# Conditioning weights by feature group, small vectors in one piece: a two-block transformer kernel on one core

## The chip, the core and the metric

The kernel runs on one core of a Trainium2 chip. The core has a matrix engine (TensorE, PE in the profile), a vector engine (VectorE, DVE), an activation engine (ScalarE, ACT), a general one (GpSimd, POOL) and SyncE (SP), which only issues transfers. ACT and POOL can issue transfers as well. The metric is the device time of one execution in microseconds. Three runs of the kernel before gave 2118.53, 2122.41 and 2126.63 us; the median is 2122.41.

## The reference

The reference computes two transformer blocks over 1024 tokens of 1024 features, in float32. What the change touches is the conditioning of the first block, ahead of everything else:

```
c_act = silu(c)                                   # one row of 1024
ada = c_act @ w_ada + b_ada                       # 1024 x 3072
shift, scale, gate = split(ada, 3)
h = rms_norm(x) * (1 + scale) + shift             # every projection of block one reads h
p = h @ w_in                                      # then GLA, HGRN, stick-breaking attention
x = x + gate * (mix(p) @ w_out)
```

Block two has sliding-window attention and an mLSTM behind a causal convolution, a cross attention to 256 memory rows, and a mixture of 32 experts with a router, from about 1440 us on. Small vectors (norm weights, biases, convolution taps, router weights) are needed at several places.

## The kernel before

Tokens go through in two halves of 512. Features lie on the partitions: the half's normalised rows are transposed into eight tiles `xraw` of 128 features x 512 tokens, and each is scaled and shifted with one column of `scc` and `shc` (features on partitions, so a conditioning value is one number per partition). The products are exact to more than one matrix pass: each operand is split into a rounded high part and a remainder (`whi`, `wlo` for weights, `fs` with `hi` and `lo` for features), and `mm3` makes three matmuls of them.

The head of the kernel does the following.

- The mask temporaries (`mk`, built by POOL and VectorE in a loop) are made and released; the pool `adp` of the conditioning weights then takes that memory.
- Four tiles `xt` of 128 token rows are loaded. Each is squared and summed by ACT (`junk<-xt`), POOL makes the reciprocal root (`rstd`), VectorE scales the rows, TensorE transposes, ACT copies to `xraw`.
- The conditioning weights for shift and scale come in 16 tiles `wa` of 512 KB, in G = 2 groups of 512 features. A tile holds 128 of the 1024 inputs on its partitions. VectorE multiplies each by `cs` (silu of c) and accumulates into `acc`; TensorE then sums over the partitions with a column of ones; two small VectorE operations add the biases into `shc` and `scc` (`cols<-mm` in the profile).
- Per feature tile, ACT writes the high part, POOL scales `xraw` in place, VectorE subtracts for the low part.
- TensorE then runs the low-rank gate projection (`lr`, L705 and L706, 16 matmuls of 512 columns) and the first of the projection slabs, each 24 matmuls.

The memory rows and the next half's token rows are loaded into the same four `xt` buffers once TensorE has transposed the first ones; they are scaled on VectorE too, far ahead of their use. A projection slab (`raw`, 512 KB, two buffers) is loaded by SyncE, rounded by ACT and subtracted by VectorE. `mmb` gives one of two PSUM banks in turn, for conditioning sums, the low-rank projection and slabs alike. The conditioning gate is computed later, in front of the first output projection, from eight loads of `w_ada` into the two `raw` buffers.

The order on each engine isn't written out: a scheduler with a timeline of its own sets it from data dependences and priorities, up to the expert stage, whose order is given by hand. Each engine and each transfer queue takes its instructions in that order. A transfer also waits for the one that used its completion semaphore before (eight of them, in turn).

## Time and profile before

| | us |
|---|---|
| median of three runs | 2122.41 |
| the profiled execution | 2122.66 |
| its span | 2120.9 |
| TensorE busy | 1942.5 (92%) |
| VectorE busy | 1475.0 (70%) |
| ACT busy | 1177.2 (56%) |
| POOL busy | 689.2 (32%) |

The span is what the trace covers; 1.8 us of the profiled execution lie around it. The busy share is a mean over stages: in the first 50 us TensorE is busy for 13.15 us, in the expert stage (1500 to 2040 us) without a break. So a stage has to be read by itself, and there it counts which wait ends last. Times in rows are microseconds from the start of the span.

### The profile page before, as it was taken

Reading aid. Unit: us, or ns where it says so; the run is one execution under the profiler, and the core shown is the slowest. Engines: PE = TensorE matmul, PEld = TensorE weight load, DVE = VectorE, ACT = ScalarE, POOL = GpSimd, SP = SyncE. Lnnn points to the kernel's source line nnn. Section 1 sums busy time; section 2 is a strip of 40 time slices with the busy share of each in tenths; the row PEclk is TensorE's granted clock in tenths of the full one; section 3 lists DMA queues with packets and bytes.
Section 4 is the critical chain, followed back from the end, with each engine's and each line's share of the span. In section 5 each row is a group of like instructions: output and inputs, shape, how many; then the busy total and the mean of one; then the engine's idle time right before and its main releaser. Section 6 shows DMA issues by size and latency. Waiting matters only on the chain.

```text
span 2120.9 us, 33031 instructions
## 1 busy us (share of the span) xinstructions
PE 1942.5 (92%) x12914; PEld 1644.2 (78%) x12914; DVE 1475.0 (70%) x1955; ACT 1177.2 (56%) x1868; POOL 689.2 (32%) x554
## 2 busy tenths in 40 slices
PE   3999899999999999999999998995999999999980
PEld 2878796887777998889888897894788888888860
DVE  6476774546777754677557755745888888888865
ACT  3454552445555543465435633652777777777852
POOL 3362110035354100242004300003455555555535
PEclk8999999999998999999999999996999999999995
DMA  9211334621011253211722156454899999999956
GB/s 294 76 51 51 112 97 128 208 73 48 22 50 31 61 156 118 70 50 61 208 60 60 51 149 232 149 219 154 343 382 384 373 378 368 371 372 370 378 195 243
DMA packets 218934, 381.61 MB, mean 180 GB/s; under 512 B 50164, under 2 KB 173076, under 8 KB 193176
## 3 DMA queue, kind: packets, MB, share of 16 engines
q1 hardware_dynamic: 194520, 345.79, 47.1%
q10 hardware_dynamic: 15040, 16.89, 2.3%
q0 software_dynamic: 9216, 16.80, 2.1%
q8 instruction: 102, 1.67, 0.3%
q14 instruction: 56, 0.46, 0.1%
HBM read 356.35 MB, written 39.85 MB: 187 GB/s over the span
## 4 chain that ended last, share of the span: by engine, by line
PE 76%; DVE 8%; DMA 5%; POOL 4%; issue 4%; ACT 3%; POOLq 0%; ACTq 0%; SPq 0%; DVEq 0%; another core or an unknown queue 0%
PE mm L133 11%; PE mm L134 11%; PE mm L135 11%; PE gu L134 6%; PE gu L133 5%; PE gu L135 5%; PE yo L135 3%; PE yo L133 3%; PE yo L134 3%; PE tp L189 3%; PE tpe L189 2%; DMA xp<-u_d 1%; PE sc L1139 1%; PE sc L1168 1%; PE at L599 1%
## 5 line engine op out<-in xcount | busy, mean ns | idle before, releaser
L43 DVE TENSOR_TENSOR elo<-eraw,ehi 128x2048 fp32r<-128x2048 f32 x192 | 429.6, 2263 | 81.1 <-ACT ehi L40 81.0
L40 ACT ACTIVATE ehi<-eraw 128x2048 fp32r<-128x2048 f32 x192 | 367.1, 1913 | 18.5 <-PE yo L135 12.5
L133 PE MATMUL mm<-whi,fs 128*128 128x256 f32 x1152 | 334.2, 292 | 1.9 <-ACT whi L40 1.9
L134 PE MATMUL mm<-wlo,fs 128*128 128x256 f32 x1152 | 333.4, 290 | 0.9 <-DVE wlo L43 0.8
L135 PE MATMUL mm<-whi,fs 128*128 128x256 f32 x1152 | 330.0, 288 | 0.0
L43 DVE TENSOR_TENSOR wlo<-raw,whi 128x1024 fp32r<-128x1024 f32 x156 | 197.3, 1266 | 149.8 <-ACT whi L40 143.5
L40 ACT ACTIVATE whi<-raw 128x1024 fp32r<-128x1024 f32 x156 | 164.8, 1056 | 214.6 <-PE mm L134 89.6
L43 POOL TENSOR_TENSOR elo<-eraw,ehi 128x1024 fp32r<-128x1024 f32 x64 | 188.2, 2941 | 230.4 <-ACT ehi L40 230.4
L133 PEld LDWEIGHTS mm<-whi,fs 128*128 128x128 f32 x1152 | 224.1, 195 | 10.2 <-issue 5.5
L134 PEld LDWEIGHTS mm<-wlo,fs 128*128 128x128 f32 x1152 | 224.4, 195 | 8.4 <-issue 6.0
L135 PEld LDWEIGHTS mm<-whi,fs 128*128 128x128 f32 x1152 | 223.2, 194 | 2.4 <-issue 2.3
L133 PE MATMUL gu<-ehi,xh 128*128 128x512 f32 x512 | 208.3, 407 | 2.5 <-ACT ehi L40 2.5
L134 PE MATMUL gu<-elo,xh 128*128 128x512 f32 x512 | 205.3, 401 | 1.5 <-DVE elo L43 1.5
L133 PE MATMUL mm<-fs,whi 128*128 128x512 f32 x480 | 195.5, 411 | 7.9 <-DVE mst L43 3.3
L135 PE MATMUL gu<-ehi,xl 128*128 128x512 f32 x512 | 202.4, 395 | 0.0
L134 PE MATMUL mm<-fs,whi 128*128 128x512 f32 x480 | 195.2, 407 | 1.2 <-DVE fs L52 1.2
L135 PE MATMUL mm<-fs,wlo 128*128 128x512 f32 x480 | 194.2, 405 | 0.0
L133 PEld LDWEIGHTS mm<-fs,whi 128*128 128x128 f32 x480 | 93.0, 194 | 38.9 <-issue 8.9
L133 PEld LDWEIGHTS gu<-ehi,xh 128*128 128x128 f32 x512 | 96.9, 189 | 24.7 <-ACT ehi L40 2.9
L135 PEld LDWEIGHTS gu<-ehi,xl 128*128 128x128 f32 x512 | 96.7, 189 | 22.9
L134 PEld LDWEIGHTS gu<-elo,xh 128*128 128x128 f32 x512 | 97.0, 190 | 22.0 <-DVE elo L43 2.2
L135 PEld LDWEIGHTS mm<-fs,wlo 128*128 128x128 f32 x480 | 93.2, 194 | 23.1 <-issue 4.0
(467 smaller groups left out, 4235.7 us busy)
## 6 DMA issues: line engine op xcount, KB each, us to landing
eraw<-in_w_e_up_dram SPq DMA_DIRECT2D x64, 1024.0 KB, 8.3
eraw<-in_w_e_down_dram SPq DMA_DIRECT2D x64, 1024.0 KB, 8.8
eraw<-in_w_e_gate_dram SPq DMA_DIRECT2D x64, 1024.0 KB, 8.6
raw<-in_w_in_dram SPq DMA_DIRECT2D x92, 512.0 KB, 3.8
raw<-in_w_out_dram SPq DMA_DIRECT2D x32, 512.0 KB, 3.5
wa<-in_w_ada_dram SPq DMA_DIRECT2D x16, 512.0 KB, 5.9
fy<-y_d SPq DMA_DIRECT2D x8, 1024.0 KB, 13.5
xt<-in_x_dram SPq DMA_DIRECT2D x8, 512.0 KB, 6.6
```

Of the source, the lines that this page charges most:

```text
L40: act.activation(out=o, in_=i, func=f, **kw)
L43: (eng or dve).tensor_tensor(out=o, in0=a, in1=b, op=op)
L133: pe.matmul(out=o, lhsT=l[0], rhs=r[0], start=start, stop=False)
L134: pe.matmul(out=o, lhsT=l[0], rhs=r[1], start=False, stop=False)
L135: pe.matmul(out=o, lhsT=l[1], rhs=r[0], start=False, stop=stop)
L189: pe.transpose(o[0:s.shape[-1], j * 128:j * 128 + s.shape[0]], s, ident[0:s.shape[0], 0:s.shape[0]])
L599: pe.matmul(out=ov[:, hh, ch], lhsT=full[:, hh, ch], rhs=v(ch, hh), start=True, stop=s0 is None)
L1139: pe.matmul(out=sc[g][:, jj * 256:jj * 256 + w], lhsT=q[r, j + jj, t * 128:(t + 1) * 128], rhs=k_full[r, k0:k0 + w], start=True, stop=True)
L1168: pe.matmul(out=os_[:, hh * 64:hh * 64 + 64], lhsT=pt[:, i * 128:(i + 1) * 128], rhs=v_full[:, kt, 64 * g:64 * g + 64], start=(hd == 0 and ...
```

## The change

Inputs are laid out on the host in another form, as part of passing them in; the kernel's arithmetic is the same, only the sum over the conditioning inputs is done in another order. The parts:

- Small vectors come packed: `small` (54 columns) in the first load of SyncE, `small_mix` and `small_router` later, instead of one transfer each.
- The token rows `xt` of the first half are issued by ACT.
- The conditioning weights lie by feature group, G = 4 groups of 256 features, in 8 transfers of 1 MB with 8 KB in a row per partition. They and the token rows get high priority, and two kinds of transfers are held behind the last of them (`issue_after`).
- The shift half is summed by TensorE (weights as the stationary operand, `cs` as one column, 64 matmuls); VectorE sums the scale half alone, in pieces of 256 columns.
- Two of the four token tiles are scaled by ACT; the last two feature tiles are scaled in place by VectorE instead of POOL.
- The gate third of the conditioning weights, the mLSTM gate weights and the router weights are contiguous per load.

```diff
-            sp.dma_start(out=xt, in_=src[rows_of(h, t), :])
+            (eng or sp).dma_start(out=xt, in_=src[rows_of(h, t), :])
...
-                sp.dma_start(out=xp, in_=src[rs, cs_].rearrange("(a p) n -> p a n", p=128))
+                with tc.issue_after(ada_last[-1]) if (h, kind) == (0, 0) else nullcontext():
+                    sp.dma_start(out=xp, in_=src[rs, cs_].rearrange("(a p) n -> p a n", p=128))
...
-    cc = vec_cols(c[0], 8)
+    cc = vec("c")
...
-    G = 2
+    G = GROUPS
...
-                sp.dma_start(out=rv, in_=kview(w_ada[0])[:, k0:k0 + 2, 2048 + n * 512:2048 + (n + 1) * 512])
+                sp.dma_start(out=rv, in_=w_ada_gate[n, :, k0:k0 + 2])
...
-        x0 = load_rows(x[0], 0)
-        was = []
-        for g in range(G):
-            was.append([])
-            for i in range(8):
-                raw = adp.tile([128, 2, 1024 // G], F32, name="wa", tag="wa", bufs=8 * G)
-                sp.dma_start(out=raw, in_=w_ada[0, i * 128:(i + 1) * 128, 0:2048].rearrange(
-                    "p (a k n) -> k p a n", a=2, k=G)[g])
-                was[-1].append(raw)
+        was, ada_last = [], []
+        with tc.high_priority():
+            x0 = load_rows(x[0], 0, eng=act)
+            for g in range(G):
+                for i in range(0, 8, 4):
+                    raw = adp.tile([128, 4, 2, 1024 // G], F32, name="wa", tag="wa", bufs=2 * G)
+                    ada_last.append(sp.dma_start(out=raw, in_=w_ada[g, :, i:i + 4]).ins)
+                    was += [raw[:, k] for k in range(4)]
         xraw = []
-        for x_ in x0:
-            TS(x_, x_, rstd_of(x_, D, junk_tile()), MUL)
+        for t, x_ in enumerate(x0):
+            r = rstd_of(x_, D, junk_tile())
+            if t < 2:
+                TS(x_, x_, r, MUL)
+            else:
+                A(x_, x_, AF.Copy, scale=r)
...
             if j == 0:
-                acc = adp.tile([128, 2, 1024 // G], F32, name="acc", tag="acc", bufs=2)
+                o = mmb()
+                for jj in range(gk):
+                    for i in range(8):
+                        pe.matmul(out=o[:, jj:jj + 1], lhsT=was[k // gk * 8 + i][:, 0, jj * 128:(jj + 1) * 128],
+                                  rhs=cs[:, i:i + 1], start=(i == 0), stop=(i == 7))
+                acc = adp.tile([128, 1024 // G], F32, name="acc", tag="acc", bufs=2)
                 for i in range(8):
-                    w = was[k // gk][i]
+                    w = was[k // gk * 8 + i][:, 1]
                     if i:
                         STT(acc, w, cs[:, i:i + 1], acc, MUL, ADD)
                     else:
                         TS(acc, w, cs[:, 0:1], MUL)
-                o = mmb()
-                for a in range(2):
-                    for jj in range(gk):
-                        pe.matmul(out=o[:, a * gk + jj:a * gk + jj + 1], lhsT=acc[:, a, jj * 128:(jj + 1) * 128],
-                                  rhs=ones, start=True, stop=True)
+                for jj in range(gk):
+                    pe.matmul(out=o[:, gk + jj:gk + jj + 1], lhsT=acc[:, jj * 128:(jj + 1) * 128], rhs=ones,
+                              start=True, stop=True)
...
-            TS(xraw[k], xraw[k], scc[:, k:k + 1], MUL, shc[:, k:k + 1], ADD, eng=pool)
+            TS(xraw[k], xraw[k], scc[:, k:k + 1], MUL, shc[:, k:k + 1], ADD,
+               eng=pool if k < 6 else dve)
...
-    sp.dma_start(out=fnw, in_=final_norm_w.partition_broadcast(128))
-    for a_, v_ in ((nmx, norm_mix_2), (ncr, norm_cross_2)):
-        sp.dma_start(out=a_, in_=v_[0].rearrange("(k p) -> p k", p=128))
+    with tc.issue_after(ada_last[-1]):
+        sp.dma_start(out=fnw, in_=final_norm_w.partition_broadcast(128))
...
-        sp.dma_start(out=wr[:, :, 0:4], in_=kview(w_router_group_2[0]))
-        sp.dma_start(out=wr[:, :, 4:36], in_=kview(w_router_expert_2[0]))
-        brow = cr.tile([128, 36], F32, name="brow")
-        sp.dma_start(out=brow[:, 0:4], in_=b_router_group_2[0].partition_broadcast(128))
-        sp.dma_start(out=brow[:, 4:36], in_=b_router_expert_2[0].partition_broadcast(128))
-        nffc = cr.tile([128, 8], F32, name="nffc")
-        sp.dma_start(out=nffc, in_=norm_ffn_2[0].rearrange("(k p) -> p k", p=128))
+        sp.dma_start(out=wr, in_=w_router)
+        sm3 = cr.tile([128, sum(n for _, n in SMALL_ROUTER)], F32, name="sm3")
+        sp.dma_start(out=sm3, in_=small_router)
+        small_v.update(vecs_of(sm3, SMALL_ROUTER))
+        brow, nffc = vec("router"), vec("norm_ffn")
```

The scheduler moves instructions with it. First SyncE's queue at the start of the program; before (`xt` token or memory rows, `wa` conditioning weights, `raw` slabs, `fnw` a norm weight, `xp` token pieces for the output projection):

```order
L91 DMA cols<-in_c_dram 128x8x1
L267 DMA xt<-in_x_dram 128x1024 x4
L117 DMA raw<-in_w_in_dram 128x8x128
L91 DMA cols<-in_norm_mem_dram 128x8x1
L421 DMA wa<-in_w_ada_dram 128x2x512 x16
L117 DMA raw<-in_w_in_dram 128x8x128 x2
L864 DMA fnw<-in_final_norm_w_dram 128x1024
L866 DMA cols<-in_norm_mix_dram 128x8x1
L866 DMA cols<-in_norm_cross_dram 128x8x1
L289 DMA xp<-in_x_dram 128x2x256 x2
L886 DMA cols<-in_norm_att_out_dram 128x4x1
L887 DMA cols<-in_norm_ml_out_dram 128x4x1
```

and now:

```order
L80 DMA cols<-in_small_dram 128x54
L124 DMA raw<-in_w_in_dram 128x8x128
L425 DMA wa<-in_w_ada_dram 128x2048 x8
L877 DMA fnw<-in_final_norm_w_dram 128x1024
L297 DMA xp<-in_x_dram 128x2x256 x2
L124 DMA raw<-in_w_in_dram 128x8x128 x2
L274 DMA xt<-in_mem_dram 128x1024 x2
L274 DMA xt<-in_x_dram 128x1024 x2
L124 DMA raw<-in_w_in_dram 128x8x128
```

The small vectors are gone from between; the memory rows and two of the next token rows stand right behind two slabs. (Before, they stood six small loads further down.)

Second, what the first wa transfers wait for, on SyncE; before:

```order
L117 DMA raw<-in_w_in_dram 128x8x128 [waits DMAHW2_49]
L91 DMA cols<-in_norm_mem_dram 128x8x1 [waits DMAHW4_49]
L421 DMA wa<-in_w_ada_dram 128x2x512 [waits DMAHW6_49,DVE_49,Pool_49]
L421 DMA wa<-in_w_ada_dram 128x2x512 [waits DMAHW0_49]
L421 DMA wa<-in_w_ada_dram 128x2x512 [waits DMAHW2_49]
```

and now:

```order
L80 DMA cols<-in_small_dram 128x54
L124 DMA raw<-in_w_in_dram 128x8x128
L425 DMA wa<-in_w_ada_dram 128x2048 [waits DMAHW1_49,DVE_49,Pool_49]
L425 DMA wa<-in_w_ada_dram 128x2048 [waits DMAHW2_49]
L425 DMA wa<-in_w_ada_dram 128x2048 [waits DMAHW3_49]
```

The wait of the first wa for VectorE and POOL is there in both.

Third, VectorE around the last group's conditioning sum (`acc` the sum, `cols<-mm` shift and scale of a group, `fs<-xraw` a low part, `xt<-xt,rstd` the scaling of memory or token rows); before:

```order
L52 SCALAR_TENSOR_TENSOR acc_337<-wa_215,cols_67,acc_337 128x1024 [waits DMAHW0_49,DVE_49]
L43 TENSOR_TENSOR wlo_459<-raw_456,whi_458 128x1024 [waits DMAHW1_49,Activation_49]
L43 TENSOR_TENSOR cols_67<-mm_346,cols_67 128x4 [waits PE_49]
L52 SCALAR_TENSOR_TENSOR cols_67<-mm_346,cols_67 128x4
L43 TENSOR_TENSOR fs_357<-xraw4_278,fs_357 128x512 [waits Pool_49]
L43 TENSOR_TENSOR fs_361<-xraw5_285,fs_361 128x512 [waits Pool_49]
L43 TENSOR_TENSOR fs_365<-xraw6_292,fs_365 128x512 [waits Pool_49]
L43 TENSOR_TENSOR fs_369<-xraw7_299,fs_369 128x512 [waits Pool_49]
L47 TENSOR_SCALAR xt_1880<-xt_1880,rstd_1887 128x1024 [waits DMAHW6_49,Activation_49,Pool_49]
L47 TENSOR_SCALAR xt_1882<-xt_1882,rstd_1894 128x1024 [waits DMAHW7_49,Activation_49,Pool_49]
L47 TENSOR_SCALAR xt_3524<-xt_3524,rstd_3535 128x1024 [waits DMAHW0_49,Activation_49,Pool_49]
L47 TENSOR_SCALAR xt_3526<-xt_3526,rstd_3542 128x1024 [waits DMAHW1_49,Activation_49,Pool_49]
```

and now:

```order
L41 TENSOR_TENSOR wlo_516<-raw_513,whi_515 128x1024 [waits DMAHW4_49,Activation_49]
L50 SCALAR_TENSOR_TENSOR acc_409<-wa_192,cols_67,acc_409 128x256 [waits DVE_49]
L41 TENSOR_TENSOR cols_67<-mm_354,cols_67 128x2 [waits PE_49]
L50 SCALAR_TENSOR_TENSOR cols_67<-mm_354,cols_67 128x2
L45 TENSOR_SCALAR xt_1936<-xt_1936,rstd_1943 128x1024 [waits DMAHW6_49,Activation_49,Pool_49]
L45 TENSOR_SCALAR xt_1938<-xt_1938,rstd_1950 128x1024 [waits DMAHW7_49,Activation_49,Pool_49]
L41 TENSOR_TENSOR fs_384<-xraw4_255,fs_384 128x512 [waits Pool_49]
L41 TENSOR_TENSOR fs_388<-xraw5_262,fs_388 128x512 [waits Pool_49]
L45 TENSOR_SCALAR xt_3580<-xt_3580,rstd_3591 128x1024 [waits DMAHW0_49,Activation_49,Pool_49]
L45 TENSOR_SCALAR xt_3582<-xt_3582,rstd_3598 128x1024 [waits DMAHW1_49,Activation_49,Pool_49]
L41 TENSOR_TENSOR cols_67<-mm_392,cols_67 128x2 [waits PE_49]
L50 SCALAR_TENSOR_TENSOR cols_67<-mm_392,cols_67 128x2
```

The four scalings of xt stood behind all conditioning work; now they stand ahead of the last group's shift and scale (`mm_392`), and the last accumulation of that group stands behind a slab's split (`wlo_516`).

## Rows read from the trace of the kernel before

**Rows 1.** The page's chain that ended last, shares by engine.
```profile
PE 76%; DVE 8%; DMA 5%; POOL 4%; issue 4%; ACT 3%; POOLq 0%; ACTq 0%; SPq 0%; DVEq 0%; another core or an unknown queue 0%
```

**Rows 2.** Head by stretches: busy us (count) per engine, granted clock, DMA share, GB/s.
```profile
15.00:20.00 5.00, 0.69 (x2) 0.29 (x2) 3.66 (x4) 4.91 (x8) 2.78 (x4) 1.00 1.05 341
...
25.00:30.00 5.00, 4.00 (x18) 2.99 (x18) 5.00 (x8) 2.77 (x5) 0.00 (x0) 1.00 1.05 385
...
45.00:50.00 5.00, 3.99 (x18) 3.73 (x19) 2.32 (x4) 0.05 (x1) 0.00 (x0) 0.50 0.79 227
```

**Rows 3.** The same table for four later stretches.
```profile
500.00:700.00 200.00, 185.96 (x1490) 150.11 (x1489) 148.17 (x223) 111.22 (x216) 90.65 (x81) 0.91 0.14 38
...
770.00:780.00 10.00, 10.00 (x85) 10.00 (x85) 5.73 (x7) 5.17 (x12) 0.52 (x1) 1.00 0.54 135
...
1264.00:1268.00 4.00, 1.97 (x17) 1.95 (x17) 3.02 (x7) 1.94 (x6) 0.00 (x0) 1.00 0.67 209
...
1500.00:2040.00 540.00, 540.00 (x2503) 437.83 (x2502) 468.04 (x300) 426.13 (x329) 286.77 (x118) 1.00 0.97 374
```

**Rows 4.** Timeline of SyncE's transfers, head: start, us of issuing, queue, line.
```profile
9.10 16.99 SPq L421 DMA_DIRECT2D wa<-in_w_ada_dram  x16
...
45.13 0.83 SPq L267 DMA_DIRECT2D xt<-in_mem_dram  x2
46.07 0.84 SPq L267 DMA_DIRECT2D xt<-in_x_dram  x2
```

**Rows 5.** Timeline of VectorE, head: start, us.
```profile
8.05 0.29 DVE L47 TENSOR_SCALAR lmask<-tf,sf 128x128 uint8<-128x128 f32 x1
...
49.71 0.15 DVE L52 SCALAR_TENSOR_TENSOR cols<-mm,cols 128x4 f32<-128x4 f32 x1
```

**Rows 6.** Groups of instructions in 0 to 70 us: busy, mean ns | idle before.
```profile
L52 DVE SCALAR_TENSOR_TENSOR acc<-wa,cols,acc 128x1024 f32<-128x1024 f32 x14 | 18.7, 1341 | 0.1
L47 DVE TENSOR_SCALAR xt<-xt,rstd 128x1024 f32<-128x1024 f32 x8 | 7.2, 898 | 5.0 <-POOL rstd L43 5.0
...
L43 POOL TENSOR_TENSOR rstd<-rstd,cols 128x1 f32<-128x1 f32 x8 | 7.0, 879 | 0.6
L47 POOL TENSOR_SCALAR rstd<-ss 128x1 f32<-128x1 f32 x8 | 4.8, 602 | 15.2 <-ACT junk L40 14.7
...
L40 ACT ACTIVATE junk<-xt 128x1024 bf16<-128x1024 f32 x8 | 8.4, 1054 | 0.3
...
L40 ACT ACTIVATION_READ_ACCUMULATOR junk<-xt 128x1 f32 x8 | 1.5, 187 | 0.0
```

**Rows 7.** Timeline of TensorE, 49 to 61 us.
```profile
49.45 0.61 PE L705 MATMUL mm<-fs,wl 128*32 128x512 f32 x1
...
52.85 0.56 PE L133 MATMUL mm<-fs,whi 128*128 128x512 f32 x1
...
60.49 1.98 PE L712 MATMUL tp<-lrs,w 32*128 32x512 f32 x4
```

**Rows 8.** Chain that ended last, in order of time: start, us, what.
```profile
344.34 3.71 DMA raw<-in_w_ada_dram
...
1256.83 6.71 DMA xp<-u_d
...
1269.45 4.51 DMA xp<-u_d
```

**Rows 9.** DMA issues: line, queue, count, KB each, median us to landing.
```profile
raw<-in_w_in_dram SPq DMA_DIRECT2D x92, 512.0 KB, 3.8
...
wa<-in_w_ada_dram SPq DMA_DIRECT2D x16, 512.0 KB, 5.9
```

**Rows 10.** Timeline, first attention round: scores on TensorE, copy back on VectorE.
```profile
73.96 0.49 PE L741 MATMUL z<-kc_full,qc 64*128 64x128 f32 x2
...
83.29 0.29 DVE L767 COPY pt<-tp 128x128 f32<-128x128 f32 x1 [1.09 <-PE tp L189]
```

More of the change, by code (lines that the diff above doesn't have):

```diff
@@ L1 @@
 import math
-from contextlib import ExitStack
+from contextlib import ExitStack, nullcontext
 import concourse.bass as bass
@@ L79, in block_kernel @@
     make_identity(nc, ident)
-    cols = const.tile([128, 128], F32, name="cols")
-    ncol = [0]
+    n_small = sum(n for _, n in SMALL)
+    cols = const.tile([128, n_small + 40], F32, name="cols")
+    sp.dma_start(out=cols[:, 0:n_small], in_=small)
+    ncol = [n_small]
     def col(n):
@@ L86, in col, with vecs_of, vec @@
         return a
-    def vec_cols(v, n, eng=None):
-        a = col(n)
-        (eng or sp).dma_start(out=a, in_=v.rearrange("(k p) -> p k", p=128))
-        return a
+    def vecs_of(t, names):
+        o, v = 0, {}
+        for name, n in names:
+            v[name] = t[:, o:o + n]
+            o += n
+        return v
+    small_v = vecs_of(cols, SMALL)
+    def vec(name):
+        return small_v[name]
     st = mkpool("st")
@@ L258, in rows_of, with load_rows @@
         return slice(h * HALF + t * 128, h * HALF + (t + n) * 128)
-    def load_rows(src, h, n=4, tag="xt", bufs=4, p=None, after=None):
+    def load_rows(src, h, n=4, tag="xt", bufs=4, p=None, after=None, eng=None):
         xr = []
@@ L883, in block_kernel @@
     a2 = mkpool("a2", a2_stack)
-    nco = col(8)
-    sp.dma_start(out=nco[:, 0:4], in_=norm_att_out_2[0].rearrange("(k p) -> p k", p=128))
-    sp.dma_start(out=nco[:, 4:8], in_=norm_ml_out_2[0].rearrange("(k p) -> p k", p=128))
-    cvb = vec_cols(conv_b_2[0], 8)
-    cvw = a2.tile([128, 4, 8], F32, name="cvw")
-    for j in range(4):
-        sp.dma_start(out=cvw[:, j], in_=conv_w_2[0, j].rearrange("(k p) -> p k", p=128))
-    bgt = col(1)
-    pool.memset(bgt, 0.0)
-    sp.dma_start(out=bgt[0:4], in_=b_gates_2[0, 0:4].rearrange("(p o) -> p o", o=1))
-    sp.dma_start(out=bgt[32:36], in_=b_gates_2[0, 4:8].rearrange("(p o) -> p o", o=1))
-    sinks = col(8)
-    sp.dma_start(out=sinks, in_=att_sinks_2[0].partition_broadcast(128))
+    sm2 = a2.tile([128, sum(n for _, n in SMALL_MIX)], F32, name="sm2")
+    sp.dma_start(out=sm2, in_=small_mix)
+    small_v.update(vecs_of(sm2, SMALL_MIX))
+    nco, cvb, bgt, sinks = vec("norm_out"), vec("conv_b"), vec("gates"), vec("sinks")
+    cvw = vec("conv_w").rearrange("p (j k) -> p j k", j=4)
     wg = a2.tile([128, 8, 64], F32R, name="wg")
@@ new lines, with _laid_out, cols, rows @@
+SMALL_MIX = [("norm_out", 8), ("conv_b", 8), ("conv_w", 32), ("gates", 1), ("sinks", 8)]
+SMALL_ROUTER = [("norm_ffn", 8), ("router", 36)]
+GROUPS = 4
+def _laid_out(inputs):
+    import numpy as np
+    a = {k: np.asarray(v) for k, v in inputs.items()}
+    def cols(v):
+        return v.reshape(-1, 128).T
+    def rows(v):
+        return np.broadcast_to(v.reshape(1, -1), (128, v.size))
+    gates = np.zeros((128, 1), np.float32)
+    gates[0:4, 0], gates[32:36, 0] = a["b_gates_2"][0, 0:4], a["b_gates_2"][0, 4:8]
+    vecs = {
+        "c": cols(a["c"][0]), "b_shift": cols(a["b_ada"][0, 0:1024]), "b_scale": cols(a["b_ada"][0, 1024:2048]),
+        "gla_gate": cols(a["b_gla_gate"][0]), "gla_norm": cols(a["gla_norm_w"][0]),
+        "hgrn_norm": np.concatenate([a["hgrn_norm_w"][0]] * 2)[:, None], "hgrn_lb": cols(a["hgrn_lb_logits"][0]),
+        "norm_mem": cols(a["norm_mem_2"][0]), "norm_mix": cols(a["norm_mix_2"][0]),
+        "norm_cross": cols(a["norm_cross_2"][0]),
+        "norm_out": np.concatenate([cols(a["norm_att_out_2"][0]), cols(a["norm_ml_out_2"][0])], 1),
+        "conv_b": cols(a["conv_b_2"][0]), "conv_w": np.concatenate([cols(v) for v in a["conv_w_2"][0]], 1),
+        "gates": gates, "sinks": rows(a["att_sinks_2"][0]), "norm_ffn": cols(a["norm_ffn_2"][0]),
+        "router": rows(np.concatenate([a["b_router_group_2"][0], a["b_router_expert_2"][0]])),
+    }
+    def slices(w):
+        return w.reshape(-1, 128, w.shape[1]).transpose(1, 0, 2)
+    ada = a["w_ada"][0].reshape(8, 128, 3, 1024)
+    ml = np.zeros((128, 8, 64), np.float32)
+    ml[:, :, 0:4], ml[:, :, 32:36] = (slices(a["w_in_2"][0][:, c0:c0 + 4]) for c0 in (2816, 2820))
+    t = {
+        "small": np.concatenate([vecs[n] for n, _ in SMALL], 1),
+        "small_mix": np.concatenate([vecs[n] for n, _ in SMALL_MIX], 1),
+        "small_router": np.concatenate([vecs[n] for n, _ in SMALL_ROUTER], 1),
+        "w_lr": slices(a["w_in"][0][:, 1024:1040]),
+        "w_ml_gates": ml,
+        "w_router": slices(np.concatenate([a["w_router_group_2"][0], a["w_router_expert_2"][0]], 1)),
+        "x": a["x"],
+        "w_ada": ada[:, :, 0:2].reshape(8, 128, 2, GROUPS, -1).transpose(3, 1, 0, 2, 4),
+        "w_ada_gate": ada[:, :, 2].reshape(8, 128, 2, 512).transpose(2, 1, 0, 3),
+    }
+    for n in ("b_ada", "w_in", "w_gla_gate2", "w_out", "final_norm_w", "mem_2", "w_in_2", "w_out_2", "w_cq_2",
+              "w_ckv_2", "w_co_2", "norm_ffn_2"):
+        t[n] = a[n]
+    for n in ("w_e_gate_2", "w_e_up_2", "w_e_down_2"):
+        w = a[n][0]
+        t[n] = w.reshape(w.shape[0], 2, -1, 128, w.shape[2]).transpose(0, 1, 3, 2, 4).reshape(w.shape[0], 2, 128, -1)
+    t["norm_final_2"] = a["norm_final_2"]
+    return t
@@ L1718 @@
     arrays, args = {}, []
[L1719 to L1724 removed]
+    for name, a in _laid_out(inputs).items():
         a = _np.ascontiguousarray(a)
```

42 lines of the change are left out of this document (13 added, 29 removed).

## Prediction

> **What bounds the kernel now.** I read the chain of waits first. TensorE carries 76% of it [rows 1], so a cut counts only where TensorE stands still. The table by stretches then says where that is: at the head, where it does little before 50 us. There I read three timelines. VectorE's [rows 5] ends the wait: the second half of the conditioning sums is turned into shift and scale at 49.71 us, after a sum that VectorE ran alone. TensorE's [rows 7] answers to it: the 16 low-rank matmuls (L705, L706) start at 49.45, the first projection slab (L133) at 52.85, the gate expansion (L712) at 60.49. SyncE's [rows 4] shows what was loaded meanwhile: 16 conditioning transfers from 9.10, the memory rows at 45.13, two of the next token rows at 46.07.
>
> **The head: what goes.** Before, VectorE sums both halves: 16 accumulations over 1024 elements at 1.28 to 1.34 us [rows 6], some 20 us, and they end last. Now it sums the scale half, 32 over 256 elements. A quarter of 1.34 is 0.34, so 32 x 0.34 = 11 us, and the shift half becomes 64 small matmuls, on a TensorE that idles. If these sums were all, the head would end right behind the last conditioning bytes.
>
> **The head: what is late next.** Two orders decide.
>
> First, "ahead of the other loads" is not quite what happens. The first wa transfer waits for VectorE and POOL in both kernels (the ordering rows with waits), because its buffer lies where the mask temporaries were. The mask loop ended at 8.05 + 0.29 = 8.34 us [rows 5] and the first wa went out at 9.10 [rows 4]. The new kernel has the same loop with a few 0.15 us operations more, so I put its first wa at 9.3.
>
> Second, VectorE's new order puts the last group's shift and scale (cols<-mm, near L41 and L50) behind four scalings of xt: two of memory rows, two of the next half's token rows. Before, those four stood behind the conditioning tail. On SyncE these rows are queued behind all of wa, then fnw, two xp and two weight slabs. VectorE takes its instructions in order, so the last group waits for a transfer that has nothing to do with it.
>
> When do they land? In units of 512 KB [rows 9] there are 16 units of wa, then fnw 1, two xp of 256 KB together 1, slabs 2, memory 2, tokens 2: 24 units, 24 x 0.524 = 12.58 MB. The rate is between 341 GB/s (15 to 20 us) and 385 (25 to 30 us) [rows 2]. I take 374, which the expert stage holds for 540 us with the 1 MB, 8 KB-a-row transfers that wa now has [rows 3]. That is 33.6 us. A lone 512 KB slab lands after 3.8 us [rows 9], of which 1.4 are bytes, so 2.1 to 2.4 us are fixed; with 2.1 the last token rows land at 9.3 + 2.1 + 33.6 = 45.0.
>
> Behind that: ACT squares 1.05 and reads the sum 0.19, POOL makes the root in 0.60 + 0.88, VectorE scales in 0.75 to 0.90 [rows 6], then two operations of 0.15: 3.9 us with the gaps. Shift and scale of the last group stand at 49.0, against 49.86 before. That is 0.9 us and not the 10 that the shorter sum suggests.
>
> What TensorE has done by then is the other half of the gain. Before, 40 matmuls of 512 columns (16 low-rank, 24 of slab one) lay between 49.45 and 60.49 [rows 7]. The slab can't start earlier now either, since its bank is the one that the last group's shift and scale are read from. But the low-rank matmuls of the first six features (12 of 16) can, in the gaps. 28 remain. The clock was granted at half (1.2 GHz) in 45 to 50 us [rows 2], after a stretch of idling, and 8 matmuls took 49.45 to 52.85, the other 32 took 7.64, 0.24 each. With the same slow start 28 take 3.4 + 20 x 0.24 = 8.2 us, with a full clock 6.7. So L712's successor comes at 57.2 instead of 60.49: 3.3 us gained. Its bounds: 385 GB/s and a full clock give 1.0 + 1.5 more, 5.8; 341 GB/s puts the rows 3.3 us later and leaves 0. A loss would need less than 341 over all 12.58 MB, which the stretches with a full queue don't show.
>
> By the Trainium skill, "DMA: Bandwidth & Descriptors", section Specifications, HBM gives one core about 358 GB/s; the 385 of [rows 2] is above it, so the trace does not agree over 5 us, and the measurement decides. By the Trainium skill's number the 24 units take 35.1 us, and the head would gain 1.8 instead of 3.3.
>
> The part moved to other engines hides: two token tiles scaled by ACT instead of VectorE (1.1 us each, long before 45), two xraw by VectorE instead of POOL at about half of 0.90. The last low parts stand near 52, and TensorE needs them as the 16th of its 28, at about 54. x on ACT's queue changes nothing that ends last. Should ACT's issue hold its first exponentials back, the cost falls into the 9 us before the first wa.
>
> **The small vectors.** At the head 17 small loads (seven on ACT, ten on SyncE) become one. Most lay between 31 and 45 us, beside VectorE's sum, so their removal is inside the sum above (a denser queue). The convolution taps and the mLSTM gate weights are loaded in one piece each instead of four and two; TensorE is busy throughout where that happens (770 to 780 us, [rows 3]): 0. The gate weights now lie in 4 KB runs instead of 2 KB: the chain waits there for landings of 3.71 us [rows 8]. A slab with 512 B runs lands in 3.8 [rows 9], so run length hardly moves it: 0, bounds -0.6 and +0.3. At the router the five loads of scattered pieces stood ahead of a load of xp that took 6.71 us on the chain; the next took 4.51 [rows 8]. The difference is 2.2, and TensorE was idle for 2.0 of the 4 us right behind it [rows 3]: I take 2.0, bounds 0 and 3.
>
> **The order behind.** The scheduler also deals out the attention of both halves anew. Of 500 to 700 us TensorE is busy 185.96, idle 14 [rows 3]. No row of before says whether that grows or shrinks. I take 0; bounds from half of it gained, 7, to as much lost.
>
> **Sum.** Profiled execution 2122.66 us (span 2120.9, 1.8 around it), 0.25 above the median of 2122.41. Minus 3.3 (head), minus 2.0 (router) = 2117.4; I say 2117.
>
> **Rivals.**
> A, nothing holds the last group. If the token and memory rows come early, or their scalings wait for little, shift and scale follow the last wa: 9.3 + 2.1 + 8.39 MB / 0.374 = 33.8, plus the last accumulation, a slab split of 1.2 and two small operations, 36. Forty matmuls in 11 us end at 47 instead of 60.5: 13.5 gained, with the router 2107. For it: the tail of sums is indeed short. Against it: the order of VectorE's rows, which is fixed.
> B, the head gains nothing: at 341 GB/s the rows land 3.3 us later, and 2120.6 is left with the router's 2. For it: 341 in 15 to 20 us [rows 2], in the midst of the same loads. The Trainium skill's 358 leans this way.
> C, the new order behind the head helps: 7 of the 14 idle us go, 2110.
> D, it becomes slower. In the stick-breaking attention one round from scores (z) through ACT, POOL and VectorE to the copy back (pt) took from 73.96 to 83.58, 9.6 us, covered by projection matmuls in between [rows 10]. If the new order leaves two such rounds of the second half uncovered, 19 us are added: 2136. It decides from 16 us on, where it eats the 5.3 and 10.6 more. For it: 14 us already stand open there. Against it: the order ranks the same priorities as before.
>
> **How the numbers follow.** No change within 0.5% (10.6 us) is what a measurement of this kernel can't tell from none: 2111.8 to 2133.0. My forecast has 0.45 (2113 to 2121 by its own bounds), A 0.19, B 0.14, C 0.12, D 0.10. A and C are faster, with a little of the forecast's edge: 0.33. D is slower: 0.10. The rest 0.57. The range: 2103 leaves out the lower part of A with a good order on top, 2128 leaves out D.
>
> **What would show it.** Right, if the first wa is issued near 9.3, the last token rows' scaling on VectorE stands right before the last cols<-mm, that pair runs at 47 to 51 us, and L712's successor starts at 55 to 59. Wrong, if that pair runs before 40 (rival A), or if the first wa goes out near 5. For the router: xp's first load lands in under 5 us. If the time between the head and 700 us differs by more than 5 us, the order behind decided and not the steps above.

## The result and the profile after

The changed kernel takes 2136.56 us (median of 8 runs, 2131.93 to 2140.62), the kernel before beside it 2125.90 (8 runs, 2118.53 to 2130.36). The ratio is 1.0057, 95% interval 1.0039 to 1.0076: slower by 0.6%, where 2117 was forecast. The profiled run is the slowest of the 8, 2140.62 us, so its trace stands 17.5 us over that of before where the medians differ by 10.7. Below, what is compared over runs uses two numbers that each run lists: its span and the mean granted clock. Span x clock is the time that the program would need at full clock; span x (1 - clock) is what it gave up to the clock. The trace keeps TensorE's clock as a list of entries, and where it has none the views print 1.00. In the changed kernel the entries begin at 54.0 us, in the kernel before at 29.3. So both numbers count as full clock whatever ran earlier in the head; behind the head every trace has entries without a gap.

The head first. SyncE's timeline of the changed kernel (start, us of issuing, queue, line; `...` marks left-out lines here and below) answers to [rows 4]:

```profile
8.36 4.40 SPq L425 DMA_DIRECT2D wa<-in_w_ada_dram  x8
...
32.57 2.97 SPq L274 DMA_DIRECT2D xt<-in_mem_dram  x2
35.63 0.86 SPq L274 DMA_DIRECT2D xt<-in_x_dram  x2
```

The first wa waits for the mask loop, as forecast (9.3 forecast, 8.36 measured). VectorE's timeline answers to [rows 5] (in brackets: idle time before, and who ended it):

```profile
42.82 0.16 DVE L41 TENSOR_TENSOR cols<-mm,cols 128x2 f32<-128x2 f32 x1 [0.76 <-PE mm L460]
...
42.96 1.57 DVE L45 TENSOR_SCALAR xt<-xt,rstd 128x1024 f32<-128x1024 f32 x2
...
49.48 1.91 DVE L45 TENSOR_SCALAR xt<-xt,rstd 128x1024 f32<-128x1024 f32 x1 [0.77 <-POOL rstd L41]
51.31 0.14 DVE L41 TENSOR_TENSOR cols<-mm,cols 128x2 f32<-128x2 f32 x1
```

Shift and scale of the last group do stand right behind the last row, at 51.31 (forecast 49.0). TensorE's timeline, which answers to [rows 7], shows that it came no earlier there:

```profile
34.97 6.96 PE L450 MATMUL mm<-cols,wa 128*128 128x1 f32 x32
41.79 0.99 PE L460 MATMUL mm<-ones,acc 128*128 128x1 f32 x4
42.65 6.96 PE L450 MATMUL mm<-cols,wa 128*128 128x1 f32 x32
49.47 0.99 PE L460 MATMUL mm<-ones,acc 128*128 128x1 f32 x4
50.33 0.61 PE L717 MATMUL mm<-fs,wl 128*32 128x512 f32 x1
...
54.32 0.39 PE L717 MATMUL mm<-fs,wl 128*32 128x512 f32 x1
```

The shift sums (L450) go on until 49.6, 6.96 us for a group of 16 matmuls. Each matmul is two passes, that is two records of the trace, 0.2175 us apart. The low-rank matmuls (L717, L718) that were to fill gaps stand behind all of them. The successor L724 starts at 61.30, where 57.2 was forecast and 60.49 was before [rows 7]. The groups of 5 to 60 us price the sums (busy, mean ns of one), of TensorE and of VectorE:

```profile
L450 PE MATMUL mm<-cols,wa 128*128 128x1 f32 x128 | 27.9, 347 | 0.6 <-DMA wa<-in_w_ada_dram 0.6
...
L50 DVE SCALAR_TENSOR_TENSOR acc<-wa,cols,acc 128x256 f32<-128x256 f32 x28 | 14.8, 527 | 1.8 <-DMA wa<-in_w_ada_dram 0.9
```

Then the whole program by stretches, cut at both halves' gate expansions, at the start of block two and at the experts (busy us of PE, PEld, DVE, ACT, POOL with counts; granted clock, DMA share, GB/s). Before:

```profile
0.00:60.49 60.49, 23.64 (x104) 16.83 (x105) 38.70 (x79) 24.74 (x43) 24.34 (x41) 0.86 0.87 263
60.49:422.71 362.22, 344.29 (x2974) 292.52 (x2973) 227.09 (x353) 171.72 (x338) 81.24 (x86) 0.97 0.35 105
422.71:829.00 406.29, 388.56 (x3086) 328.06 (x3085) 266.57 (x398) 203.67 (x391) 130.29 (x128) 0.93 0.26 72
829.00:1472.40 643.40, 602.98 (x4076) 535.78 (x4074) 408.76 (x789) 307.54 (x730) 120.09 (x156) 0.97 0.37 116
1472.40:2120.90 648.50, 583.01 (x2680) 470.99 (x2680) 533.90 (x339) 469.51 (x370) 333.28 (x145) 0.95 0.90 345
```

and after:

```profile
0.00:61.30 61.30, 49.06 (x217) 43.17 (x217) 35.99 (x101) 26.92 (x45) 19.74 (x40) 1.00 0.70 259
61.30:428.73 367.43, 346.93 (x2974) 295.51 (x2973) 226.44 (x350) 171.32 (x338) 77.27 (x84) 0.96 0.34 103
428.73:846.60 417.87, 398.91 (x3086) 335.74 (x3085) 267.18 (x398) 203.18 (x391) 129.18 (x126) 0.91 0.24 70
846.60:1490.50 643.90, 604.89 (x4076) 537.92 (x4075) 408.80 (x789) 308.02 (x730) 120.30 (x156) 0.97 0.37 116
1490.50:2138.40 647.90, 582.70 (x2680) 470.76 (x2680) 533.40 (x339) 469.23 (x370) 332.19 (x145) 0.95 0.90 345
```

The head costs 0.8 us more, the first half's mixer 5.2, the second half's 11.6, the rest nothing. In the second half's mixer TensorE has the same 3086 records, and its idle time is 17.7 us before and 19.0 after: hardly any wait has come in. It is busy for longer, at a lower clock: 406.29 x 0.93 = 378 and 417.87 x 0.91 = 380. One place of it, changed kernel, by stretches:

```profile
690.00:692.00 2.00, 2.00 (x13) 1.59 (x12) 2.00 (x3) 1.11 (x3) 2.00 (x2) 1.00 0.01 4
692.00:706.00 14.00, 14.00 (x51) 11.25 (x51) 12.66 (x18) 7.87 (x20) 9.72 (x9) 0.51 0.01 2
706.00:708.00 2.00, 2.00 (x20) 2.00 (x18) 1.97 (x3) 2.00 (x5) 1.88 (x1) 1.00 0.10 9
```

and on its TensorE timeline the same score matmul at full clock and in this stretch, with what ran as the clock fell:

```profile
674.92 1.12 PE L753 MATMUL z<-kc_full,qc 64*128 64x512 f32 x2
...
691.95 0.43 PE L611 MATMUL at<-vv,stf 128*128 128x64 f32 x2
692.93 0.69 PE L611 MATMUL at<-vv,stf 128*128 128x64 f32 x2
...
699.76 2.07 PE L753 MATMUL z<-kc_full,qc 64*128 64x512 f32 x2
```

The clock is at its lower level (1.2 of 2.4 GHz) for 14 us, after a row of state matmuls of 64 columns. The kernel before has such drops too, at the same work, but shorter:

```profile
684.00:692.00 8.00, 8.00 (x37) 7.39 (x37) 6.10 (x11) 3.74 (x13) 5.44 (x5) 0.57 0.01 3
```

The rows show what TensorE does before the clock comes back. Before, the state matmuls (sixteen rows) follow projection matmuls without a gap. The clock fell at 684.6, and the last four rows ran slower; projection matmuls of 256 columns followed from 688.66, and it was back at 691.5. After, they follow a wait of 1.69 us for VectorE, and nine of the sixteen rows ran slower, then also a score and transposes; the projection matmuls came only from 702.53, and the clock was back at 706. First before, then after:

```profile
684.54 0.61 PE L599 MATMUL at<-vv,stf 128*128 128x64 f32 x2
...
688.66 0.56 PE L133 MATMUL mm<-whi,fs 128*128 128x256 f32 x1
```

```profile
689.80 0.41 PE L611 MATMUL at<-vv,stf 128*128 128x64 f32 x2 [1.69 <-DVE Sb L50]
...
702.53 0.56 PE L142 MATMUL mm<-whi,fs 128*128 128x256 f32 x1
```

That what stands between the fall and the projection matmuls makes the drop longer is argued from these rows; no run shows it.

In steps of 1 us, both second mixers have nine drops. Before, none gives up more than 5.1 us, 28.8 in all; after, three give up 6.8 each (494 to 508, 692 to 706, 743 to 758), 39.9 in all. These are single profiles, and drops vary from run to run: the changed kernel's second profile (run 12) has eight there, two of 6.8, 35.8 in all.

### The profile page after: what moved, and what is told of

Read it like the earlier page. It is cut to its first block, busy times and chain, and to the rows that moved or that the text cites. A ratio compares the mean times of both kernels' runs of the same rounds, so it can differ in the third digit from the quotient of the medians.

```text
span 2138.4 us, 33217 instructions
## 1 busy us (share of the span) xinstructions
PE 1982.5 (93%) x13026; PEld 1683.1 (79%) x13026; DVE 1471.8 (69%) x1975; ACT 1178.7 (55%) x1870; POOL 678.7 (32%) x550
## 3 DMA queue, kind: packets, MB, share of 16 engines
q8 instruction: 103, 1.69, 0.3%
## 4 chain that ended last, share of the span: by engine, by line
PE 78%; DVE 8%; DMA 5%; POOL 3%; ACT 3%; issue 3%; POOLq 0%; SPq 0%; ACTq 0%; DVEq 0%; another core or an unknown queue 0%
PE mm L140 11%; PE mm L141 11%; PE mm L142 11%; PE gu L142 5%; PE gu L141 5%; PE gu L140 5%; PE tp L196 3%; PE yo L142 3%; PE yo L140 3%; PE yo L141 3%; PE tpe L196 2%; PE z L753 1%; PE sc L1140 1%; PE mm L450 1%; PE at L611 1%
## 5 line engine op out<-in xcount | busy, mean ns | idle before, releaser
L38 ACT ACTIVATE ehi<-eraw 128x2048 fp32r<-128x2048 f32 x192 | 366.9, 1912 | 18.8 <-PE yo L142 12.7
L141 PE MATMUL mm<-wlo,fs 128*128 128x256 f32 x1152 | 337.8, 294 | 1.5 <-DVE wlo L41 1.5
L140 PE MATMUL mm<-whi,fs 128*128 128x256 f32 x1152 | 337.2, 294 | 0.9 <-ACT whi L38 0.7
L142 PE MATMUL mm<-whi,fs 128*128 128x256 f32 x1152 | 335.3, 293 | 0.0
L141 PEld LDWEIGHTS mm<-wlo,fs 128*128 128x128 f32 x1152 | 228.6, 198 | 11.6 <-issue 7.8
L140 PEld LDWEIGHTS mm<-whi,fs 128*128 128x128 f32 x1152 | 227.7, 198 | 8.6 <-issue 5.1
L142 PEld LDWEIGHTS mm<-whi,fs 128*128 128x128 f32 x1152 | 227.7, 198 | 6.0 <-issue 5.9
```

The lines of the kernel that those rows point to most:

```text
L38: act.activation(out=o, in_=i, func=f, **kw)
L140: pe.matmul(out=o, lhsT=l[0], rhs=r[0], start=start, stop=False)
L141: pe.matmul(out=o, lhsT=l[0], rhs=r[1], start=False, stop=False)
L142: pe.matmul(out=o, lhsT=l[1], rhs=r[0], start=False, stop=stop)
```

## The experiments

Theory 1: the shift sums hold the head, on TensorE. Theory 2: the rest of the loss is the new order behind the head. Where the text says how far two orders agree, it is the share of TensorE's matmuls in a half's mixer that have the same name (without buffer numbers) at the same place in both traces. Clock numbers are means over the runs; the head's end (gate expansion) and its share of what was given up to the clock (stretch x (1 - clock)) are from the profile. "None" stands where the trace has no clock entry until 53 to 58 us, which is so in all five profiles with the shift half summed by one moving column; in the other nine the entries begin at 18 to 31 us. "Before" pools its 92 runs beside runs 1 to 12, and "changed" 15 runs; ratios are to the runs of before on the same chip.

| run | median us | ratio (95%) | head ends | span x clock | given up, head + behind |
|---|---|---|---|---|---|
| before | 2124.8 | | 60.49 | 2020.5 | 8.5 + 93.8 |
| changed | 2136.0 | | 61.30 | 2031.9 | none + 101.6 |
| 1 VectorE sums | 2120.53 | 0.9991 (0.9971-1.0010) | 56.03 | 2012.2 | 11.8 + 94.5 |
| 2 same, with another order | 2125.12 | 1.0003 (0.9989-1.0017) | 55.71 | 2013.3 | 13.9 + 95.5 |
| 3 rows on ACT | 2136.14 | 1.0058 (1.0040-1.0076) | 61.61 | 2031.8 | none + 102.5 |
| 4 token rows without priority | 2127.45 | 1.0013 (1.0000-1.0027) | 65.67 | 2033.1 | none + 91.0 |
| 5 free loads, TensorE sums | 2132.96 | 1.0045 (1.0026-1.0065) | 65.16 | 2031.9 | none + 99.3 |
| 6 free loads, VectorE sums | 2125.95 | 1.0007 (0.9988-1.0026) | 60.52 | 2014.0 | 13.9 + 95.5 |
| 7 VectorE sums, two groups | 2120.15 | 0.9986 (0.9971-1.0001) | 60.70 | 2014.8 | 13.4 + 90.0 |
| 8 row sum | 2115.28 | 0.9965 (0.9947-0.9984) | 49.38 | 2015.3 | 0 + 98.7 |
| 9 row sum, rows on ACT | 2122.48 | 0.9977 (0.9959-0.9996) | 51.77 | 2019.9 | 0 + 99.8 |
| 10 row sum, free loads | 2132.85 | 1.0034 (1.0018-1.0051) | 53.40 | 2025.0 | 0 + 106.8 |
| 11 before, two rows on ACT | 2136.64 | 1.0054 (1.0035-1.0073) | 61.71 | 2023.1 | 10.5 + 101.2 |
| 12 changed again | 2135.96 | 1.0043 (1.0018-1.0068) | 60.93 | 2032.4 | none + 100.2 |

**Run 1**, the sum back on VectorE:

```diff
...
-                        pe.matmul(out=o[:, jj:jj + 1], lhsT=was[k // gk * 8 + i][:, 0, jj * 128:(jj + 1) * 128],
-                                  rhs=cs[:, i:i + 1], start=(i == 0), stop=(i == 7))
-                acc = adp.tile([128, 1024 // G], F32, name="acc", tag="acc", bufs=2)
+                acc = adp.tile([128, 2, 1024 // G], F32, name="acc", tag="acc", bufs=2)
...
```

> The changed kernel, but VectorE sums both halves again (32 accumulations over 512 elements); TensorE has no shift matmuls. The second half's attention keeps the changed kernel's order. Theory 1 (TensorE holds the head: 64 shift matmuls are 128 passes of 0.2175 us, 27.8 us, and the last group's and the low-rank matmuls stand behind them): the last shift and scale move from 51.3 to about 44, the first gate expansion starts at 53 to 55 instead of 61.30. Rival (the rows that VectorE scales ahead of the last group hold the head, as the prediction had it): also earlier here, since the scalings now stand behind the conditioning, so this run prices the sum and the third separates the two. Theory 2 (the new order of the second half's attention costs 10 to 11 us): its mixer, from the second half's gate expansion to the eight transposes behind it, stays at 324 us (before 313.3, changed 324.0). Total 2136.6 - 7 = 2129. If the sum is the whole loss, and the order is not one, 2118 or less.

VectorE's timeline has shift and scale at 45.30, the head ends at 56.03, 5.3 us earlier. The total fell by more than the head, to 2120.5: what is given up behind it is 94.5, not 101.6, although 90% of the second half's order is the changed kernel's (81% of the first half's). Theory 2 missed here.

```profile
45.30 0.15 DVE L41 TENSOR_TENSOR cols<-mm,cols 128x2 f32<-128x2 f32 x1
...
46.93 0.75 DVE L45 TENSOR_SCALAR xt<-xt,rstd 128x1024 f32<-128x1024 f32 x1
```

**Run 2**, on top of it:

```diff
-            if t < 2:
+            if t < 4:
...
-            TS(x_, x_, r, MUL)
+            A(x_, x_, AF.Copy, scale=r)
...
-            TS(xt, xt, r, MUL)
+            A(xt, xt, AF.Copy, scale=r)
```

> As the first, and the token rows of the first half are all scaled by VectorE, those of the memory and of the next half by ACT. The scheduler then deals out the second half's attention as in the kernel before (its last score matmul stands 906 instructions behind its first; before 883, changed 1006). Theory 2: the second half's mixer takes 313 to 315 us, 10 less than in the first run, at a like head (first gate expansion at 53 to 56). Total 2118 to 2120. Rival (the mixer is slower for its transfers or for a lower granted clock, not for its order): it stays at 324, total 2129.

The stretch of the second half's mixer is 412.1 us against 412.8 in run 1: no gain from this order by itself, a miss. On TensorE the second half's order is that of run 4, matmul for matmul, and agrees with the kernel before in 70%.

**Run 3**, the changed kernel with the last two of these edits alone (the next half's token rows, and the memory rows):

```diff
-            TS(x_, x_, r, MUL)
+            A(x_, x_, AF.Copy, scale=r)
...
-            TS(xt, xt, r, MUL)
+            A(xt, xt, AF.Copy, scale=r)
```

> The changed kernel with the shift sums on TensorE, but ACT scales the memory rows and the next half's token rows, so that no row stands ahead of the last group's shift and scale on VectorE. Theory 1: TensorE still ends its sums at 50.4, the last shift and scale come at 50.5 to 51, the first gate expansion at 60 to 61 (now 61.30). Rival (VectorE's rows hold it): shift and scale right behind the last weights and sums, at 42 to 45, the gate expansion at 52 to 55. The last score matmul stands 936 instructions behind its first: by theory 2 the second half's mixer takes about 317, between both kernels. Total by theories 1 and 2: 2128 to 2131; by the rival 2121 to 2124.

No row stands ahead on VectorE now, and nothing is gained: it waits 3.74 us for TensorE, and the gate expansion comes at 61.61. The head is TensorE's; the rows that the prediction put there would have held the last group only 0.9 us longer (51.31 against 50.46).

```profile
42.85 0.15 DVE L50 SCALAR_TENSOR_TENSOR cols<-mm,cols 128x2 f32<-128x2 f32 x1
50.46 0.16 DVE L41 TENSOR_TENSOR cols<-mm,cols 128x2 f32<-128x2 f32 x1 [3.74 <-PE mm L460]
50.53 0.15 DVE L50 SCALAR_TENSOR_TENSOR cols<-mm,cols 128x2 f32<-128x2 f32 x1
```

**Run 4**:

```diff
-        with tc.high_priority():
-            x0 = load_rows(x[0], 0, eng=act)
+        x0 = load_rows(x[0], 0, eng=act)
+        with tc.high_priority():
```

> The changed kernel with the shift sums on TensorE, but without high priority for the token rows (the conditioning weights keep it). The scheduler deals out the second half's attention as in the kernel before (last score matmul 906 behind the first); at the head two slabs go out ahead of the conditioning weights and the token rows come later. Theory 2: the second half's mixer takes 313 to 315 us. Theory 1: the TensorE sums still take 28 us, so the head is no better: first gate expansion at 61 to 64. Total 2126 to 2129. Rival (transfers or clock, not order): mixer at 324, total 2137 or more.

The first half has the order of before (99.9%); the second agrees with it in 70%, where the changed kernel does in 50%. 91.0 us are given up behind the head instead of 101.6, at a head 4.4 us longer; the second half's mixer takes 407.1 us. Its drops are ten, none over 3.4 us.

**Runs 5 and 6**, the changed kernel and run 1 with

```diff
-    with tc.issue_after(ada_last[-1]):
+    with nullcontext():
```

at both places: one order behind the head (100% and 99.7%), two ways to sum.

> The changed kernel, shift sums on TensorE, without the two issue_after (a norm weight and two xp pieces, 1 MB, go out ahead of the conditioning weights). It is one of a pair: this kernel and the next have the same order of instructions on all engines behind the head, and differ in who sums the shift half. What is to be told apart: behind the head the changed kernel lost 102.7 us to a granted clock below full (span x (1 - mean clock), mean of its runs), the kernel with VectorE's sums 94.5. Theory (order): where the gaps of TensorE fall decides how often the clock drops, so a pair of one order loses the same behind the head, within the 5 us that single runs scatter, and differs by the head alone, 5 us. Rival (carry-over): a TensorE kept busy for 28 us in the head costs clock later: this one loses 8 us more behind the head than its pair and is 13 to 16 us slower. This kernel by the theory: first gate expansion at 61 to 63, 2130 to 2138; by the rival 2133 to 2140.

> The other of the pair: VectorE sums both halves, without the two issue_after, same order behind the head. First gate expansion at 56 to 58. Theory (order): 5 us faster than its pair, and as much lost behind the head. Rival (carry-over): 13 to 16 us faster than its pair, 2120 to 2124.

They differ by 7.0 us, 4.6 of it in the head. Given up behind it: 99.3 and 95.5, whose means are uncertain by 1 and 2 (run to run 3.7 and 7.0, 12 runs each). Nearer to the order than to the carry-over, not decided by itself.

**Run 7**, run 6 with

```diff
-               eng=pool if k < 6 else dve)
+               eng=pool)
...
-GROUPS = 4
+GROUPS = 2
```

> VectorE sums both halves in two groups, POOL scales all feature tiles in place, no issue_after, packed vectors and contiguous weights as in the changed kernel. Behind the head its order is that of the kernel without priority for the token rows (fourth run), which lost 91.0 us there with TensorE's sums in its head. Theory (order): 89 to 94 us lost behind the head here too; rival (carry-over): 83 to 86. The last two groups' halves end later than with four, and the four row scalings stand ahead of them again: first gate expansion at 56 to 60. Total 2114 to 2120.

Behind the head it has run 4's order and gives up 90.0 there against 91.0, with TensorE busy for 26 us of its head instead of 49. A busy head costs no clock later: the carry-over has fallen.

**Run 8**, the sum turned round:

```diff
-                        pe.matmul(out=o[:, jj:jj + 1], lhsT=was[k // gk * 8 + i][:, 0, jj * 128:(jj + 1) * 128],
-                                  rhs=cs[:, i:i + 1], start=(i == 0), stop=(i == 7))
...
+                    pe.matmul(out=orow[0:1, 0:nc_], lhsT=cs[:, i:i + 1], rhs=was[k // gk * 8 + i][:, 0], start=(i == 0),
+                              stop=(i == 7))
...
+                    pe.matmul(out=o[:, jj:jj + 1], lhsT=srow[:, jj * 128:(jj + 1) * 128], rhs=ones[0:1], start=True,
+                              stop=True)
```

> The changed kernel, with TensorE's shift sum turned round: the column of cs is the stationary operand and the weights move, 32 matmuls of 256 columns instead of 64 of one; ACT copies the row out, and two matmuls of one row turn it into columns. Theory 1 (the price of the sum is the number of passes with one column, 128 x 0.2175 us): the gate's matmuls of 512 columns take 0.47 us a pass, so 256 columns 0.235, 64 passes 15 us instead of 27.8, spread over the landing of the weights: last shift and scale at 42 to 45, first gate expansion at 52 to 56. Rival (TensorE's work of that kind costs the same by the byte of weights): 60 to 62. Total by theory 1 about 2124 to 2131 (the order behind is that of neither kernel), by the rival 2130 to 2138.

Better than expected, and faster than both kernels. The group of the same bytes takes 16.9 us instead of 27.9:

```profile
L450 PE MATMUL mm<-wa,cols 128*1 128x256 f32 x64 | 16.9, 418 | 0.5 <-DMA wa<-in_w_ada_dram 0.5
```

On its TensorE timeline the shift sums end at 37.7, and twelve low-rank matmuls run ahead of the last group's scale sum (41.56). They are some 0.23 us apart from the start, where in the changed kernel the first were 0.42 apart:

```profile
34.09 3.61 PE L450 MATMUL mm<-wa,cols 128*1 128x256 f32 x16
...
38.76 0.42 PE L723 MATMUL mm<-fs,wl 128*32 128x512 f32 x1
39.02 0.39 PE L724 MATMUL mm<-fs,wl 128*32 128x512 f32 x1
...
42.47 0.47 PE L140 MATMUL mm<-fs,whi 128*128 128x512 f32 x1 [0.41 <-DVE cols L50]
...
49.38 1.98 PE L730 MATMUL tp<-lrs,w 32*128 32x512 f32 x4 [0.20 <-ACT lrs L38]
```

By the rows most of the gain is pace. In the last two groups a pass of 256 columns takes 3.61 / 16 = 0.226 us; 64 of them would be 14.4. One column at the full clock was 0.12 in the kernel before (below), and 128 of those would be 15.6. By these two estimates both forms cost much the same at full clock; the one-column sums never reached it.

**Runs 9 and 10** are run 8 with the edits of run 3 and of run 5. They were to tell which half's order gives the clock away.

> The kernel with the row sum (eighth run), and ACT scales the memory rows and the next half's token rows. The head should stay near 49 us (48 to 51). Behind it the order is another: the first half's attention is dealt out as in the kernel before, the second half's much as in the changed kernel (last score matmul 1007 behind the first). If the first half's order decides the time lost to the clock: 90 to 94 us lost behind the head, 2106 to 2110; if the second half's does: 98 to 103, 2114 to 2119.

> The kernel with the row sum without the two issue_after: 1 MB goes out ahead of the conditioning weights, head at 52 to 54. The other way round behind it: the first half's attention as in the changed kernel, the second half's short as in the kernel before (906 behind the first). If the first half's order decides: 98 to 103 us lost behind the head, 2117 to 2123; if the second half's does: 90 to 94, 2109 to 2114.

Given up behind the head: 99.8 and 106.8. Run 9 has 98% of the changed kernel's second half and 87% of the first half of before, so its 99.8 is what was expected if the second half decides. Run 10 did not test what it was to test: its first half is the changed kernel's, but its second agrees with the kernel before in 52% only and with the changed kernel in 60%, and 106.8 lies above both expectations.

**Run 11**, the kernel before with

```diff
-        for x_ in x0:
-            TS(x_, x_, rstd_of(x_, D, junk_tile()), MUL)
+        for t, x_ in enumerate(x0):
+            r = rstd_of(x_, D, junk_tile())
+            if t < 2:
+                TS(x_, x_, r, MUL)
+            else:
+                A(x_, x_, AF.Copy, scale=r)
```

> The kernel before, with one edit that hardly touches its head: two of the four token tiles are scaled by ACT instead of VectorE. The scheduler deals out the attention of both halves anew, as in the pair without issue_after, which lost 99.3 and 95.5 us behind the head where the kernel before lost 94 (102.4 less 8.5 in the head). First gate expansion within 1 us of 60.5. If the order alone moves the time: 95 to 100 us lost behind the head, 2125 to 2130. If what moved it was something else of the change (loads, packing, the head): as before, 2122 to 2125.

Nothing of the packing, the loads or the sum is in it, and it is as slow as the changed kernel: 8.8 us over before on the same chip, 1.2 of it in the head (61.71). Span x clock is 2023.1 against 2021.5 there; given up behind the head 101.2. Its drops include three of 6.8 us (491 to 506, 686 to 701, 737 to 752), at the places of the changed kernel's. On TensorE its order is that of runs 5 and 6 (100% and 99.7% or more), and the second half is the changed kernel's (99.4%). The edit itself is two scalings on another engine; with the order that came with it, the time moves by as much as the whole loss. The amount is not fixed by TensorE's order alone: the three kernels that share it give up 95.5, 99.3 and 101.2.

**Run 12**, the changed kernel again:

> The changed kernel once more, beside the others of this call. First gate expansion at 61.3; 100 to 105 us lost to the clock, none of it in the head; 2132 to 2140, 17 to 24 us above the kernel with the row sum.

As expected, apart from the distance to run 8: 20.7 us by the medians, but the two ran on different chips, and by their ratios to the kernel before beside them it is 0.78%, 16.6 us, a little under the 17 to 24 expected.

## Why the prediction was wrong

The kernel before was itself 3.5 us slower in the eight runs beside the changed kernel (2125.90) than in the three that the forecast started from (2122.41). The other 16 us or so between 2117.4 and 2136.56 are: 4.1 in the head, 2.0 at the router, 9.9 in the order behind.

- **The first wa and the mask loop**: right, 8.36.
- **The last group behind four rows on VectorE**: the order was read rightly and the rows came at about the time forecast, but it decided nothing. Run 3 took them away and kept the head.
- **"the shift half becomes 64 small matmuls, on a TensorE that idles"**: this step failed. It was costed at nothing. The matmuls are 128 passes of 0.2175 us, 27.9 us, where the weights take some 20 us to land (8.39 MB at 423 GB/s). They set the end of the sums and push the low-rank matmuls behind them, so that the 12 that were to run "in the gaps" did not. The trace of before had two prices for such a pass that were not read:

```profile
32.53 1.95 PE L449 MATMUL mm<-ones,acc 128*128 128x1 f32 x16 [1.22 <-DVE acc L52]
...
46.01 3.58 PE L449 MATMUL mm<-ones,acc 128*128 128x1 f32 x16 [11.54 <-DVE acc L52]
```

  That is 0.12 us a pass where the granted clock is 1.00 by the trace's entries (32 to 34 us), and 0.22 where it is 0.50 (46 to 50). The sum should have had 15.6 to 28.7 us of TensorE in it; the measured 27.9 is the price at the lower level.

- **VectorE's share**: 0.34 us each was a quarter of 1.34; measured 0.527, 14.8 + 1.4 = 16.2 us with the first of each group instead of 11. The forecast was too small, but the rest is hidden behind TensorE.
- **Head**: +0.8 instead of -3.3. With VectorE's sum (run 1) it is -4.5, with the row sum -11.1.
- **Gate**: right at 0; the chain waits there for landings of 3.65 where it was 3.71 [rows 8].

```profile
341.44 3.65 DMA raw<-in_w_ada_gate_dram
```

- **Router**: the xp load lands in 3.45 on the chain instead of 6.71 [rows 8], as forecast, but the chain now comes to it through two others:

```profile
1264.63 5.65 DMA raw<-in_w_out_dram
...
1271.00 6.05 DMA x_d<-xp
1277.13 3.45 DMA xp<-u_d
```

  The stretch from the start of block two to the experts does not shrink (643.4 and 643.9). TensorE's idle time in it falls by 1.4 us and its busy time grows by 1.9: the forecast 2.0 are not seen in the time.
- **The order behind, "I take 0; bounds from half of it gained, 7, to as much lost"**: the second failed step. It was put at nothing because no row spoke for either sign. The prediction's own sign for it came: before 700 us the first half's mixer alone is 5.2 us longer. Over the runs the changed kernel's span is 10.7 us longer (2133.4 against 2122.8); 0.8 lie in the head, 9.9 behind it, and of these 101.6 - 93.8 = 7.8 are clock. The other 2.1 are what TensorE's idle time behind the head grows by in the two profiles. The bound was made of idle time, the smaller part. Rival D gave the time, 2136, by luck: its mechanism isn't there, since idle time in the second half's mixer rose by 1.2 us, not 19.

What stays open is how an order sets the size of the loss. The second half's order points the right way: where it is the changed kernel's to 97% or more (the changed kernel, runs 5, 6, 9 and 11) 95.5 to 101.6 us are given up behind the head, with three different first halves; where it is run 4's (runs 2, 4 and 7) 90.0 to 95.5. But run 1, with 90% of it, gives up 94.5, and run 10, with an order of its own, 106.8. The rows of the two drops above show more narrow matmuls between the fall of the clock and the next projection matmuls; no run shows that this sets the length.

## What to carry to other kernels

A sum on an engine that "idles" has a price and a place in that engine's order: find the nearest row of its shape, and ask what stands behind it. Price it at both levels of the clock, since here the whole row of passes ran at the lower one. Here it was faster to let the weights move and the single column stand still. Where a scheduler deals out a program anew, an edit must be judged with the order it brings: here an edit that saves nothing moved the time by 0.5%, so compare span x clock and the time given up to the clock apart before crediting a difference to the edit.
